# Hybrid decoder block: the input of the first product is loaded in column pieces and turned by TensorE instead of VectorE

## Chip, cores and metric

One core of a Trainium2 chip runs one decoder layer for 256 tokens. The metric is the device time of one execution in microseconds (us), as the median of several runs: 1473.47 us over 3 runs (1473.1 to 1473.87) before the change.

## What is computed

The reference, cut to the part that the change touches and what follows it (sizes: 256 tokens, model width 2048, w_in 2048 x 8704):

```python
u = rms_norm(h, g_mix[l])                      # h is x, (1, 256, 2048)
proj = u @ w_in[l]
q, k, v, z, gb, gc, gate_a, gate_c = jnp.split(proj, split_points, axis=-1)
q = rope(q.reshape(b, t, N_Q_HEADS, HEAD_DIM), positions)
k = rope(k.reshape(b, t, N_KV_HEADS, HEAD_DIM), positions)
y_attn = sliding_window_attention(q, k, v, attn_sinks[l]) @ w_attn_proj[l]
y_conv = short_gated_conv(z, gb, gc, conv_w[l]) @ w_conv_proj[l]
merged = jax.nn.sigmoid(gate_a) * y_attn + jax.nn.sigmoid(gate_c) * y_conv
h = h + merged @ w_mix_out[l]
h = h + cross_attention(rms_norm(h, g_xattn[l]), rms_norm(mem, g_mem[l]), ...)
hid = rms_norm(h, g_ffn[l]) @ w_ffn_in[l]
h = h + (silu(hid[..., :FFN_HIDDEN]) * hid[..., FFN_HIDDEN:]) @ w_ffn_out[l]
```

## The kernel before

Every weight matrix goes through the chip once, in tiles of two contraction blocks of 128 rows by 512 columns (`raw`, 512 KB, five buffers). `weights` (line 70) loads a tile on SP's queue (line 80) and `split` (line 54) cuts it into a high part on ScalarE (`whi`, line 55, a cast) and a low part on VectorE (`wlo`, line 56, a subtraction). `gemm_tf` (line 112) multiplies an activation by 512 columns of a weight, token tile by token tile: three products a contraction tile (`part`, lines 122 to 124: high x high, high x low, low x high), two token tiles, 16 contraction tiles, so 96 products of 128x512 for a matrix with 2048 rows. `gemm_ft` (line 86) gives the transposed result with two products (lines 96 and 100). The order of the instructions on each engine comes from a scheduler that runs over the program; `hooks` lets code run ahead of a given weight tile.

The activation `X1` of the first product has to hold features on the partitions, as a high and a low part, times the gain `g_mix`. Before, x is loaded by `x_in` / `stage_in` (line 227) in eight pieces of 256 KB, each for 32 partitions, such that a partition holds 32 i + b for token 32 j + b and features of block i. VectorE transposes it in squares of 32 x 32 (`feat`, line 214), and `high_low` (lines 221 and 222) makes the high part on ScalarE and the low part on VectorE. Since a partition then holds features m apart, the rows of w_in are loaded to match: `rows_pk` puts row (c P + p) m + k on partition p. `stage_rms` (lines 183 and 235 to 245) makes the tokens' 1/rms from sums of squares on ScalarE, a product with `ones` on TensorE (`ssp`, line 239) and a reduction; `spread` (line 263, tile `rw`) lays it out for later use. `evac_q` (line 297) scales the first product's result by it into `q_sb`.

Ahead of all that TensorE runs 20 matmuls of `ident` with itself (`heat`, line 167). The small constants (`rows`, `rope`, `sink` and the gains, lines 157, 159, 304, 310 and 312) are loaded on SP's queue between the weights; `rows` is turned by TensorE into `cols_ps` (line 306). The first hooks:

```python
first = {k: [lambda k=k: feat(x0, KD, k, 2, k, g_mix, X1)] for k in range(4, KD, 2)}
first[0] = [lambda: x_in(0), lambda: x_feat(0, 0), lambda: x_feat(2, 0)]
first[1] = [lambda: x_in(1), lambda: x_feat(0, 1), lambda: x_feat(2, 1)]
gemm_tf(W, KD, X1, 0, evac_q(0), hooks=first, lead=4, head=2)
```

`lead=4` makes the first four weight tiles one contraction block each (256 KB); `head=2` holds two of them and runs them token tile by token tile.

Of the kernel before, what the change touches and what calls it, by code (L numbers as in the profile page):

```python
# [17 lines left out]
P = 128  # L18
D = 2048
# [22 lines left out]
def hybrid_block(ctx, tc, a, out):  # L42
# [14 lines left out]

    def rows_kp(W):
        """Contraction tile k, partition p holds row k P + p."""
        v = W.rearrange("(k p) n -> p k n", p=P)  # L60
        return lambda k0, n: v[:, k0:k0 + n, :]

    def rows_pk(W, m):
        """Contraction tile m c + k, partition p holds row (c P + p) m + k."""
        v = W.rearrange("(c p k) n -> c p k n", p=P, k=m)
        return lambda k0, n: v[k0 // m][:, k0 % m:k0 % m + n, :]
# [19 lines left out]
    def gemm_ft(W, kt, X, c0, evac, cols=C, hooks=None):  # L86
        """[features, tokens] tiles of X.T @ W[:, c0:c0+cols]; evac first adds the two halves
        of a sum; what it does after its yield is spread over the weight tiles of the next product."""
# [23 lines left out]
    def gemm_tf(W, kt, X, c0, evac, cols=C, hooks=None, last=1, lead=0, head=1):  # L112
        """[tokens, features] tiles of X.T @ W[:, c0:c0+cols]; the first and last weight tiles go token tile by token tile."""
# [40 lines left out]
    def gain(n, m):  # L154
        o = const.tile([P, KD], F32, name=n)
        if m == KD:
            nc.sync.dma_start(o, a[n][0].rearrange("(p k) -> p k", k=m))
        else:
            nc.sync.dma_start(o.rearrange("p (c k) -> p c k", k=m), a[n][0].rearrange("(c p k) -> p c k", p=P, k=m))
        return o  # L160

    g_mix = gain("g_mix", KD)

    # keep the tensor engine's clock up while the first loads are under way
    heat = tps.tile([P, C], F32, tag="tp", name="heat")
    for i in range(20):
        nc.tensor.matmul(heat[:, :P], lhsT=ident, rhs=ident, start=True, stop=True)

    # additive masks: current block keeps key <= query, previous block key > query
# [28 lines left out]
    # A staged block holds 32 i + b on its partitions, for token 32 j + b and features (i, f):  # L198
    # transposing its 32 x 32 squares puts features on the partitions and tokens next to each other.
# [8 lines left out]
    def feat(stage, m, k0, n, kx, g, X, j0=0, nj=NJ):  # L208
        """X[:, kx + k, 0/1, tokens] = high/low parts of (stage * g) for the features f = m a + k0 + k."""
        nt = nj * Q  # L210
        xt = sp.tile([P, n, nt], F32, tag="xt", name="xt", bufs=2)
        v = stage.rearrange("p j (a k) -> p k j a", k=m)
        for k in range(n):
            nc.vector.transpose(xt[:, k, :].rearrange("p (j b) -> p j b", b=Q), v[:, k0 + k, j0:j0 + nj, :])  # L214
        high_low([xt[:, k, :] for k in range(n)], kx, g, X, slice(j0 * Q, j0 * Q + nt))
# [13 lines left out]
    def stage_rms(stage, name):  # L229
        """1/rms of the tokens of a staged block: [P, NT] by partition, and [P, T] on every partition."""  # L230
# [18 lines left out]
    def bounce(c, st, eng=nc.sync):  # L249
        """Stage column chunk c of h by way of DRAM."""  # L250
        hd = dp.tile([T, C], F32, tag="hd", name="hd")
        eng.dma_start(hd.rearrange("(t p) f -> p t f", p=P), h[:, :, c * C:(c + 1) * C])
        for i in range(P // Q):
            stage_in(st, hd, i, eng=eng)

    def spread(r, name):
        """rB[p, t*P + n] = r[n, t] on every partition p."""
# [12 lines left out]
    # ================= mixer =================  # L270
    with ExitStack() as ph:
        mp = ph.enter_context(tc.tile_pool(name="mp", bufs=1))
        ap_ = ph.enter_context(tc.tile_pool(name="ap", bufs=2))
        W = rows_pk(a["w_in"][0], KD)
        x0 = mp.tile([P, NJ, C], F32, tag="x0", name="x0")
        X1 = xp.tile([P, KD, 2, T], F32R, tag="X", name="X1")

        HJ = NJ // 2

        def x_in(th):  # L280
            for i in range(P // Q):
                stage_in(x0, a["x"][0], i, th * HJ, HJ)

        def x_feat(k0, th):
            feat(x0, KD, k0, 2, k0, g_mix, X1, th * HJ, HJ)

        first = {k: [lambda k=k: feat(x0, KD, k, 2, k, g_mix, X1)] for k in range(4, KD, 2)}
        first[0] = [lambda: x_in(0), lambda: x_feat(0, 0), lambda: x_feat(2, 0)]
        first[1] = [lambda: x_in(1), lambda: x_feat(0, 1), lambda: x_feat(2, 1)]
# [3 lines left out]
        def evac_q(c):  # L293
            def evac(t, p):
                if not r0:
                    r0.extend(stage_rms(x0, "r0B"))
# [4 lines left out]
        gemm_tf(W, KD, X1, 0, evac_q(0), hooks=first, lead=4, head=2)  # L301
        NR = 3 * KC
        rows = const.tile([NR, P], F32, name="rows")
        nc.sync.dma_start(rows, a["conv_w"][0].rearrange("j (r c) -> (j r) c", c=P))
# [5 lines left out]
        nc.sync.dma_start(rope, a["rope_table"].rearrange("(t p) s d -> p t s d", p=P))  # L310
        sink = const.tile([P, NH], F32, name="sink")
        nc.sync.dma_start(sink, a["attn_sinks"].broadcast_to([P, NH]))
# [11 lines left out]
        # rotary, in place, on GpSimd  # L324
# [20 lines left out]
        # gated short convolution, [features, tokens]  # L345
# [44 lines left out]
        # attention stages per kv head  # L390
# [26 lines left out]
        def scores(g):  # L417
            kv = g
            p_sb = ap_.tile([P, 4, 3, P], F32, tag="p_sb", name="p_sb")
            # block layout on axis 2: 0 = tile 0, 1..2 = tile 1 (previous, current)  # L420
# [92 lines left out]
        # merge  # L513
# [38 lines left out]
    # ================= cross attention =================  # L552
# [135 lines left out]
    # ================= feed-forward =================  # L688
# [98 lines left out]
```

## Time and profile before

| | |
|---|---|
| median of 3 runs | 1473.47 us (1473.1 to 1473.87) |
| span of the profiled execution | 1474.0 us (the page gives no other time of it) |
| TensorE (PE) busy | 1441.9 us, 98% |
| VectorE (DVE) busy | 886.3 us, 60% |
| ScalarE (ACT) busy | 724.0 us, 49% |
| GpSimd (POOL) busy | 46.6 us, 3% |
| DMA | 275.11 MB, mean 187 GB/s |

The profile is of one execution. Busy shares are means over the whole span; what happens in a stretch is read from the timeline and the windows of that stretch. A busy PE is one that has a matmul in it, at either of its clock levels; the granted clock stands in the windows' column PEclk. PEld is PE's weight load, SPq and POOLq are the queues that issue DMAs.

### The profile page before, as it was taken

How to read it: one execution, taken by the hardware profiler on the slowest of the kernel's cores; microseconds unless marked ns; L12 is line 12 of the kernel's file. 1: busy time of each engine (PE TensorE's matmuls, PEld its weight loads, DVE VectorE, ACT ScalarE, POOL GpSimd, SP SyncE). 2: the span in 40 equal slices, each digit the busy share in tenths (PEclk: the TensorE clock that was granted, in tenths of full speed). 3: DMA queues.
4: the chain of work that ended last, by engine and by line, in shares of the span. 5: the costliest groups of instructions: out<-in, count | busy, mean ns of one | idle time of the engine just before them, and what ended most of it. 6: DMA issues, size and time to landing. Idle time of an engine off the chain costs nothing.

```text
span 1474.0 us, 20189 instructions
## 1 busy us (share of the span) xinstructions
PE 1441.9 (98%) x7707; PEld 1227.6 (83%) x7707; DVE 886.3 (60%) x1316; ACT 724.0 (49%) x1115; POOL 46.6 (3%) x67
## 2 busy tenths in 40 slices
PE   7999999999999996999999999999999999999997
PEld 6888888888888875899888888888888888888886
DVE  6557768555557858585655656556556555545454
ACT  6443555554455545565654544545445444434343
POOL 0061000000000010000000000000000000000000
PEclk9999999999999998999999999999999999999999
DMA  8664454456656678865566665665666666555553
GB/s 227 198 188 147 145 170 148 155 176 198 191 176 192 194 204 241 254 192 163 175 186 186 186 195 183 194 188 186 193 190 184 190 193 217 187 188 189 191 188 115
DMA packets 147028, 275.11 MB, mean 187 GB/s; under 512 B 10588, under 2 KB 18804, under 8 KB 146804
## 3 DMA queue, kind: packets, MB, share of 16 engines
q1 hardware_dynamic: 145780, 269.64, 59.3%
q0 software_dynamic: 1152, 4.19, 1.2%
q8 instruction: 60, 0.98, 0.3%
q14 instruction: 36, 0.29, 0.1%
HBM read 269.60 MB, written 4.19 MB: 186 GB/s over the span
## 4 chain that ended last, share of the span: by engine, by line
PE 92%; DMA 2%; POOL 2%; DVE 2%; issue 1%; ACT 0%; ACTq 0%; POOLq 0%; SPq 0%; DVEq 0%
PE acc L96 41%; PE acc L100 21%; PE acc L123 9%; PE acc L124 9%; PE acc L122 9%; DMA mem<-in_mem 2%; DMA x<-in_x 1%; DVE xt L214 1%; PE sps L430 1%; PE ops L483 1%; DVE XM L222 0%; DVE wlo L56 0%; PE tp L472 0%; POOL sa L336 0%; POOL sa L335 0%
## 5 line engine op out<-in xcount | busy, mean ns | idle before, releaser
L56 DVE TENSOR_TENSOR wlo<-raw,whi 128x1024 fp32r<-128x1024 f32 (+1 forms) x506 | 607.0, 1205 | 527.1 <-ACT whi L55 526.9
L55 ACT CAST whi<-raw 128x1024 fp32r<-128x1024 f32 (+1 forms) x506 | 520.2, 1033 | 624.5 <-PE acc L96 359.7
L96 PE MATMUL acc<-X,whi 128*128 128x512 f32 x2368 | 805.8, 396 | 0.0
L100 PE MATMUL acc<-X,wlo 128*128 128x256 f32 x2368 | 607.3, 280 | 0.0
L96 PEld LDWEIGHTS acc<-X,whi 128*128 128x128 f32 x2368 | 435.9, 188 | 83.6 <-issue 0.8
L100 PEld LDWEIGHTS acc<-X,wlo 128*128 128x128 f32 x2368 | 446.2, 188 | 23.9 <-issue 1.1
L124 PE MATMUL acc<-whi,gT 128*128 128x512 f32 x352 | 138.9, 395 | 0.0
L123 PE MATMUL acc<-wlo,gT 128*128 128x512 f32 x352 | 138.9, 394 | 0.0
L122 PE MATMUL acc<-whi,gT 128*128 128x512 f32 x352 | 125.4, 395 | 0.0
L107 ACT COPY half<-acc 128x256 f32<-128x256 f32 x184 | 67.5, 369 | 25.5 <-PE acc L100 23.5
L122 PEld LDWEIGHTS acc<-whi,gT 128*128 128x128 f32 x352 | 66.4, 189 | 15.5
L124 PEld LDWEIGHTS acc<-whi,gT 128*128 128x128 f32 x352 | 66.3, 188 | 15.5
L123 PEld LDWEIGHTS acc<-wlo,gT 128*128 128x128 f32 x352 | 66.3, 188 | 15.4
L123 PE MATMUL acc<-wlo,MG 128*128 128x512 f32 x128 | 51.0, 399 | 12.7 <-DVE wlo L56 12.7
L124 PE MATMUL acc<-whi,MG 128*128 128x512 f32 x128 | 50.6, 395 | 0.0
L122 PE MATMUL acc<-whi,MG 128*128 128x512 f32 x128 | 45.4, 393 | 0.0
L96 PE MATMUL acc<-yc,whi 128*128 128x512 f32 x128 | 43.7, 394 | 0.0
L96 PE MATMUL acc<-oT,whi 128*128 128x512 f32 x128 | 43.5, 394 | 0.0
L122 PE MATMUL acc<-whi,X 128*128 128x512 f32 x96 | 34.4, 401 | 5.9 <-ACT whi L55 3.3
L123 PEld LDWEIGHTS acc<-wlo,MG 128*128 128x128 f32 x128 | 24.5, 192 | 18.7 <-DVE wlo L56 13.5
L123 PE MATMUL acc<-wlo,X 128*128 128x512 f32 x96 | 38.2, 403 | 0.9 <-DVE wlo L56 0.9
L124 PE MATMUL acc<-whi,X 128*128 128x512 f32 x96 | 37.6, 397 | 0.0
(189 smaller groups left out, 1106.1 us busy)
## 6 DMA issues: line engine op xcount, KB each, us to landing
raw<-in_w_ffn_in SPq DMA_DIRECT2D x176, 512.0 KB, 4.3
raw<-in_w_in SPq DMA_DIRECT2D x134, 512.0 KB, 3.8
raw<-in_w_ffn_out SPq DMA_DIRECT2D x88, 512.0 KB, 4.6
raw<-in_w_mix_out SPq DMA_DIRECT2D x32, 512.0 KB, 4.8
raw<-in_w_attn_proj SPq DMA_DIRECT2D x16, 512.0 KB, 4.3
raw<-in_w_conv_proj SPq DMA_DIRECT2D x16, 512.0 KB, 4.0
raw<-in_w_xkv SPq DMA_DIRECT2D x8, 512.0 KB, 3.9
raw<-in_w_xkv SPq DMA_DIRECT2D x16, 256.0 KB, 2.8
```

Of the source, the lines that this page charges most:

```text
L55: nc.scalar.copy(hi, src)
L56: nc.vector.tensor_tensor(out=lo, in0=src, in1=hi.bitcast(F32), op=ALU.subtract)
L96: nc.tensor.matmul(ps[m], lhsT=hi[:, k, ms], rhs=X[:, kk].rearrange("p s t -> p (s t)"), start=(kk == 0), stop=False,)
L100: nc.tensor.matmul(ps[m][:, :T], lhsT=lo[:, k, ms], rhs=X[:, kk, 0, :], start=False, stop=(kk == kt - 1),)
L107: nc.scalar.copy(t2, ps[m][:, T:])
L122: nc.tensor.matmul(o, lhsT=xh, rhs=hi[:, k, :cols], start=(kk == 0), stop=False)
L123: nc.tensor.matmul(o, lhsT=xh, rhs=lo[:, k, :cols], start=False, stop=False)
L124: nc.tensor.matmul(o, lhsT=xl, rhs=hi[:, k, :cols], start=False, stop=(kk == kt - 1))
L214: nc.vector.transpose(xt[:, k, :].rearrange("p (j b) -> p j b", b=Q), v[:, k0 + k, j0:j0 + nj, :])
L430: nc.tensor.matmul(sps[par][:, j].rearrange("p a b -> p (a b)"), lhsT=qT[b:b + 64, hh // 2, t * P:(t + 1) * P], rhs=kT[b:b + 64, sw, kv // ...
L483: nc.tensor.matmul(ops[64 * par:64 * par + 64], lhsT=v_sb[:, kb, vs], rhs=pt[:, t + kb, par::2, :], start=(kb == 0), stop=(kb == t),)
```

## The change

x is loaded with tokens on the partitions, all 128 of them, in column pieces: 256, 256, 512, 512 and 512 columns of both token tiles, each issued on SP between the first weight tiles. TensorE transposes the 128 x 128 blocks into PSUM (`x_turn`), two contraction tiles a PSUM tile, and `high_low` reads PSUM. The gain g_mix is loaded as 16 rows on ScalarE's queue and turned by TensorE as well. Sums of squares are taken from the natural layout (`x_sums`), so that `ssp` goes. w_in is read by `rows_kp`: tile k holds the neighbouring rows k P to k P + 127. `heat` has 8 matmuls instead of 20, `head=2` goes, and the other small loads move from SP's queue to GpSimd's. The rest of the kernel stays.

```diff
     def gain(n, m):
         o = const.tile([P, KD], F32, name=n)
         if m == KD:
-            nc.sync.dma_start(o, a[n][0].rearrange("(p k) -> p k", k=m))
+            nc.gpsimd.dma_start(o, a[n][0].rearrange("(p k) -> p k", k=m))
         else:
-            nc.sync.dma_start(o.rearrange("p (c k) -> p c k", k=m), a[n][0].rearrange("(c p k) -> p c k", p=P, k=m))
+            nc.gpsimd.dma_start(o.rearrange("p (c k) -> p c k", k=m), a[n][0].rearrange("(c p k) -> p c k", p=P, k=m))
         return o
-    g_mix = gain("g_mix", KD)
+    g_rows = const.tile([KD, P], F32, name="g_rows")
+    nc.scalar.dma_start(g_rows, a["g_mix"][0].rearrange("(k p) -> k p", p=P))
     heat = tps.tile([P, C], F32, tag="tp", name="heat")
-    for i in range(20):
+    for i in range(8):
         nc.tensor.matmul(heat[:, :P], lhsT=ident, rhs=ident, start=True, stop=True)
...
-        W = rows_pk(a["w_in"][0], KD)
-        x0 = mp.tile([P, NJ, C], F32, tag="x0", name="x0")
+        W = rows_kp(a["w_in"][0])
+        x0 = mp.tile([P, NT, D], F32, tag="x0", name="x0")
         X1 = xp.tile([P, KD, 2, T], F32R, tag="X", name="X1")
-        HJ = NJ // 2
-        def x_in(th):
-            for i in range(P // Q):
-                stage_in(x0, a["x"][0], i, th * HJ, HJ)
-        def x_feat(k0, th):
-            feat(x0, KD, k0, 2, k0, g_mix, X1, th * HJ, HJ)
-        first = {k: [lambda k=k: feat(x0, KD, k, 2, k, g_mix, X1)] for k in range(4, KD, 2)}
-        first[0] = [lambda: x_in(0), lambda: x_feat(0, 0), lambda: x_feat(2, 0)]
-        first[1] = [lambda: x_in(1), lambda: x_feat(0, 1), lambda: x_feat(2, 1)]
+        xn = a["x"][0].rearrange("(t p) d -> p t d", p=P)
+        ss0 = tiny.tile([P, NT, D // C], F32, tag="ss0", name="ss0")
+        g_mix = const.tile([P, KD], F32, name="g_mix")
+        def x_in(f0, f1):
+            nc.sync.dma_start(x0[:, :, f0:f1], xn[:, :, f0:f1])
+        def g_turn():
+            gp = tps.tile([P, C], F32, tag="tp", name="gp")
+            nc.tensor.transpose(gp[:, :KD], g_rows, ident[:KD, :KD])
+            nc.vector.tensor_copy(g_mix, gp[:, :KD])
+        def x_turn(k):
+            tp = tps.tile([P, 2, T], F32, tag="tp", name="tp")
+            for i in range(2):
+                for t in range(NT):
+                    nc.tensor.transpose(
+                        tp[:, i, t * P:(t + 1) * P], x0[:, t, (k + i) * P:(k + i + 1) * P], ident)
+            high_low([tp[:, i, :] for i in range(2)], k, g_mix, X1)
+        def x_sums(c):
+            for t in range(NT):
+                sumsq(x0[:, t, c * C:(c + 1) * C], ss0[:, t, c:c + 1])
+        first = {k: [] for k in (0, 1, 2, 3, 4, 6, 8, 10, 12, 14)}
+        first[0] = [lambda: x_in(0, 2 * P), g_turn, lambda: x_turn(0)]
+        first[1] = [lambda: x_in(2 * P, C), lambda: x_turn(2)]
+        first[3] = [lambda: x_in(C, 2 * C)]
+        first[4] = [lambda: x_turn(4), lambda: x_turn(6), lambda: x_in(2 * C, 3 * C)]
+        first[6] = [lambda: x_sums(0)]
+        first[8] = [lambda: x_turn(8), lambda: x_turn(10), lambda: x_in(3 * C, D)]
+        first[10] = [lambda: x_sums(1)]
+        first[12] = [lambda: x_turn(12), lambda: x_turn(14), lambda: x_sums(2)]
+        first[14] = [lambda: x_sums(3)]
...
                 if not r0:
-                    r0.extend(stage_rms(x0, "r0B"))
+                    r = rstd_sum(ss0)
+                    r0.extend((r, spread(r, "r0B")))
...
-        gemm_tf(W, KD, X1, 0, evac_q(0), hooks=first, lead=4, head=2)
+        gemm_tf(W, KD, X1, 0, evac_q(0), hooks=first, lead=4)
...
-        nc.sync.dma_start(rows, a["conv_w"][0].rearrange("j (r c) -> (j r) c", c=P))
+        nc.gpsimd.dma_start(rows, a["conv_w"][0].rearrange("j (r c) -> (j r) c", c=P))
...
-        nc.sync.dma_start(rope, a["rope_table"].rearrange("(t p) s d -> p t s d", p=P))
+        nc.gpsimd.dma_start(rope, a["rope_table"].rearrange("(t p) s d -> p t s d", p=P))
...
-        nc.sync.dma_start(sink, a["attn_sinks"].broadcast_to([P, NH]))
+        nc.gpsimd.dma_start(sink, a["attn_sinks"].broadcast_to([P, NH]))
```

The scheduler's order at the places that matter. SP's queue from the start of the program, before (x is the input tile, raw a weight tile; a row is the line, the kind and the transfer's shape):

```order
L157 DMA g_mix<-in_g_mix 128x16
L227 DMA x_129<-in_x 32x4x512 x4
L80 DMA raw<-in_w_in 128x512
L227 DMA x_129<-in_x 32x4x512 x4
L80 DMA raw<-in_w_in 128x512 x3
L80 DMA raw<-in_w_in 128x2x512
L304 DMA rows<-in_conv_w 24x128
```

and of the change:

```order
L284 DMA x_117<-in_x 128x2x256
L80 DMA raw<-in_w_in 128x512
L284 DMA x_117<-in_x 128x2x256
L80 DMA raw<-in_w_in 128x512 x2
L284 DMA x_117<-in_x 128x2x512
L80 DMA raw<-in_w_in 128x512
L284 DMA x_117<-in_x 128x2x512
L80 DMA raw<-in_w_in 128x2x512 x2
L284 DMA x_117<-in_x 128x2x512
```

The first weight tile moves from behind 1 MB of x to behind 256 KB of it, and the last piece of x to behind eight contraction tiles of weights.

ACT's queue at the same place, before (junk is a sum of squares, X a high part of the activation, whi a high part of a weight):

```order
L183 ACTIVATE junk,ssj<-x_129 128x512
L221 ACTIVATE X_130<-xt,g_mix 128x128 x2
L183 ACTIVATE junk,ssj<-x_129 128x512
L221 ACTIVATE X_130<-xt,g_mix 128x128
L55 CAST whi<-raw 128x512
```

and of the change:

```order
L55 CAST whi<-raw 128x512
L185 ACTIVATE junk,ss_119<-x_117 128x512 x2
L55 CAST whi<-raw 128x512 x2
L223 ACTIVATE X_118<-tp,g_mix 128x256 x2
L185 ACTIVATE junk,ss_119<-x_117 128x512
L223 ACTIVATE X_118<-tp,g_mix 128x256
L185 ACTIVATE junk,ss_119<-x_117 128x512
L223 ACTIVATE X_118<-tp,g_mix 128x256 x2
```

Two sums of squares and three casts now stand ahead of the first X. PE's queue of the change, from its first matmul (gp is the turned gain, tp the turned x, acc a product; before, the 20 matmuls of heat are followed by products alone):

```order
L169 MATMUL heat<-ident 128x128 x8
L288 MATMUL gp<-ident,g_rows 128x16
L295 MATMUL tp<-ident,x_117 128x128 x8
L122 MATMUL acc<-whi,X_118 128x512
L123 MATMUL acc<-wlo,X_118 128x512
L122 MATMUL acc<-whi,X_118 128x512
L123 MATMUL acc<-wlo,X_118 128x512
L295 MATMUL tp<-ident,x_117 128x128 x4
```

Eight of the 32 transposes stand ahead of the first product, the others in groups of four between the products. After the first gemm the rows of all engines are the same as before, line numbers aside.

## Rows read from the trace of the kernel before

**Rows 1.** The page: span, and the chain that ended last, by engine

```profile
span 1474.0 us, 20189 instructions
...
PE 92%; DMA 2%; POOL 2%; DVE 2%; issue 1%; ACT 0%; ACTq 0%; POOLq 0%; SPq 0%; DVEq 0%
```

**Rows 2.** Timeline of PE, first 20 us: start, duration, engine, line, what, count, [idle before]

```profile
1.53 7.20 PE L167 MATMUL heat<-ident 128*128 128x128 f32 x40 [1.53 <-POOL ident masks.py:199]
11.99 0.51 PE L122 MATMUL acc<-whi,X 128*128 128x512 f32 x1 [3.25 <-ACT whi L55]
```

**Rows 3.** Windows: stretch, length, busy time by engine, granted clock, DMA share, GB/s

```profile
15.00:20.00 5.00, 3.86 (x8) 2.34 (x9) 4.71 (x13) 4.31 (x12) 0.00 (x0) 0.50 1.06 307
...
1.53:8.73 7.20, 7.20 (x40) 1.00 0.87 193
11.99:16.14 4.15, 1.24 (x3) 0.69 1.05 286
16.14:20.20 4.06, 4.06 (x8) 0.50 1.05 273
20.20:41.10 20.90, 20.18 (x89) 1.00 0.72 228
```

**Rows 4.** Waits of the first 45 us: who, for whom, us in total, times, longest

```profile
DVE xt L214 <- DMA x<-in_x: 8.3, 1, 8.3
```

**Rows 5.** Timeline of ACT, first 45 us

```profile
11.33 0.60 ACT L55 CAST whi<-raw 128x512 fp32r<-128x512 f32 x1
12.14 0.61 ACT L183 ACTIVATE junk<-x 128x512 f32<-128x512 f32 x1
12.88 0.63 ACT L183 ACTIVATE junk<-x 128x512 f32<-128x512 f32 x1
41.56 1.27 ACT L297 ACTIVATE q_sb<-acc,rstd 128x512 f32<-128x512 f32 x2 [1.91 <-PE acc L124]
```

**Rows 6.** Timeline of PE, 36 to 45 us

```profile
36.54 0.39 PE L124 MATMUL acc<-whi,X 128*128 128x512 f32 x1
...
37.45 0.39 PE L122 MATMUL acc<-whi,X 128*128 128x512 f32 x1
...
43.34 0.39 PE L123 MATMUL acc<-wlo,X 128*128 128x512 f32 x1
...
44.06 0.50 PE L124 MATMUL acc<-whi,X 128*128 128x512 f32 x1
```

**Rows 7.** DMA: landing times of x (tile x), SP's timeline, issues of weights

```profile
DMA to landing us min/median/max: 4.2/6.5/9.7
...
1.19 1.84 SPq L227 DMA_DIRECT2D x<-in_x  x4
...
raw<-in_w_xkv SPq DMA_DIRECT2D x16, 256.0 KB, 2.8
```

**Rows 8.** Tile tp (transposes through PSUM later in the kernel) and PE's timeline there

```profile
L221 ACT ACTIVATE X<-tp,g_ffn x16: 459/472/477, 718.6 to 740.0; 128x256 fp32r<-128x256 f32 x16
L222 DVE SCALAR_TENSOR_TENSOR X<-tp,g_ffn,X x16: 473/478/485, 719.8 to 740.5; 128x256 fp32r<-128x256 f32 x16
...
717.47 1.35 PE L677 MATMUL tp<-ident,h 128*128 128x128 f32 x10
```

**Rows 9.** DMA issues on POOL's queue: KB each, median us to landing

```profile
mem<-in_mem POOLq DMA_DIRECT2D x4, 512.0 KB, 18.2
```

**Rows 10.** Timelines of POOL and DVE, 525 to 566 us

```profile
532.92 1.19 POOL L227 DMA_DIRECT2D mem<-in_mem  x2
...
559.29 2.08 DVE L214 STREAM_TRANSPOSE xt<-mem 128x256 f32<-128x256 f32 x4 [13.41 <-DMA mem<-in_mem]
```

**Rows 11.** Windows in the mixer, and DMA issues of weights (w_in by rows_pk)

```profile
50.00:100.00 50.00, 50.00 (x242) 42.04 (x241) 22.88 (x18) 22.23 (x25) 14.97 (x21) 1.00 0.62 191
...
raw<-in_w_in SPq DMA_DIRECT2D x134, 512.0 KB, 3.8
...
raw<-in_w_mix_out SPq DMA_DIRECT2D x32, 512.0 KB, 4.8
```

## Prediction

> **What bounds the kernel now.** I read the page first. Of a span of 1474.0 us, the chain that ended last is 92% TensorE (PE) [rows 1]. So a time is worth something only where PE stands still or is slowed, and the place to look is where the change is: the start. The timeline of PE's first microseconds shows it: warming matmuls ("heat") until 8.73, then nothing until the first product (a 128x512 matmul of the first gemm) at 11.99 [rows 2]. The windows show what follows: three products up to 16.14, busy 1.24 of 4.15 us, then eight in 4.06, twice the later pace. Their clock column has granted 1.00 over 1.53 to 8.73, 0.69 from 11.99 to 16.14, 0.50 (the 1.2 GHz level) from 16.14 to 20.20, and 1.00 after that [rows 3]. The waits of the first 45 us name the cause: DVE stands 8.3 us for the DMA of x [rows 4], ACT's cast of the first weight (whi) ends only at 11.93 [rows 5], and PE's first product is released by it [rows 2]. From 20.20 to 41.10 PE is busy 20.18 of 20.90 us [rows 3].
>
> How much is lost: the marker is the start of ACT's q_sb (line 297), which releases when the first product's first token tile is complete: 41.56 [rows 5]. The first gemm has 96 products up to about there (16 contraction tiles, 3 products, 2 token tiles). In the steady stretch four starts take 0.91 us, 0.2275 each [rows 6], so 96 are 21.8 us. From 11.99 to 41.56 is 29.6: 7.7 us are holes, half clock, and the two passes of the ssp product. Everything behind the marker is bound by PE in both kernels.
>
> **The change, step by step.** All of it is at the start; the order excerpts show what stands on SP, ACT and PE. Behind the first gemm, the instructions of every engine stand in the same order as before.
>
> *Loads.* Before, SP issues eight pieces of x (256 KB each, 32 partitions) around one weight tile. They land 4.2 to 9.7 us after issue, the ninth issue of 0.46 from 1.19 on ending at about 5.4, so x is complete at about 15.1, and from 1.53 to 8.73 the DMA engines move 193 GB/s at a share of 0.87; from 15 to 20, with weights alone, 307 GB/s at 1.06 [rows 3, 7]. Per share, x costs about 1.3 times as much. Now x comes over 128 partitions, as weights do, the first piece being 256 columns (256 KB). I have no row for such a piece of x. Bounds for its landing: 2.8 us (w_xkv, 256 KB over 128 partitions, same row length) and 4.2 us (the fastest piece of x before) [rows 7]. I take 3.1, near the first, because shape and bytes are those of w_xkv. Four issues on SP take 1.84, 0.46 each, from 1.19 on; x's first now takes g_mix's place, one ahead, at 0.74 [rows 7]; the pieces are then bound by their bytes at 307 GB/s, 0.85 us for 256 KB. Landings: x0 3.85, w0 4.7, x1 5.55, w1 6.4, w2 7.25, then 512 KB of x at 9.0, w3 9.8, x 11.5, w4-5 13.2.
>
> *First product.* ACT's new order decides: cast of w0, two sums of squares of x (which need x1), casts of w1 and w2, and only then X of tile 0. Cast 0.60; squares 0.74 each where they follow each other (12.14 to 12.88) [rows 5]; X from PSUM 0.472 [rows 8]. So 4.7+0.60 = 5.3; squares 5.55 to 7.05; casts to 8.25; X at 8.7; with 0.06 to PE (11.93 to 11.99 in rows 2 and 5) the first product starts at **8.8 instead of 11.99**. Heat is 8 matmuls instead of 20 (40 passes took 7.20, so 16 take some 3.2 and end by 4.9); the first eight transposes follow it and are done near 6.5, hidden under ACT's casts. If that cover were gone they would cost 8 x 0.18 = 1.4 at heat's mean pace.
>
> *PE after its first product.* 96 products 21.8. 24 more transposes of 128x128: ten of them stand between 717.47 and 718.57, 0.11 each, and I take 0.12: 2.9. The DVE's 20 transposes of x go, which PE did not pay for directly. The two transposes of the spread (rw) and cols_ps move ahead of the marker: 43.34 to 44.06 holds them and one product [rows 6], so they are 0.5, paid before the marker and saved behind it. The ssp product goes (two passes); I leave its gain as reserve against small new waits.
>
> *Waits that it adds.* X of the two columns in one PSUM tile alternates ACT 0.472 and DVE 0.478 [rows 8], about 1.0 a column; behind the first X, ACT does X, a sum of squares, X, a sum, X: X of contraction tile 3 at 8.7 + 3x0.47 + 2x0.74 = 11.6, while PE has 18 products and 4 transposes (4.6 us) before it needs that, 13.4. So short holes only: bounds 0.3 and 2.0, taken 1.0. ACT has 16 X, 8 sums, 4 short and 6 long casts, some 22 us from 4.7 on, which ends near 27 and leaves it ahead of PE.
>
> *Clock.* Before, it fell while PE had stood still for 3.3 us and then run three products, and it was back at 20.2 after products had run back to back from 16.14 [rows 2, 3]. Now PE stands still from 6.5 to 8.8 and is broken up until 12. Bounds: no loss, or a half clock for as long as before: a mean of 0.69 over 4.15 us is 2.6 us at half, and with the 4.06 behind it [rows 3] 6.6, of which half is lost, 3.3. Taken 1.6, the middle. The Trainium skill ("TensorE: Matmul & The Clock Gate", Part 4) states that transposes do not count as activity for the clock; no row before shows transposes alone at a start. By that rule the loss is the upper bound and the result 1469.7, by the middle 1468.0.
>
> *Small loads.* rows, rope, sink and three gains go to POOL's queue, where a load of 512 KB takes 18 us to land [rows 9]. The first user is cols_ps, which the new order puts among the last products of the first gemm, near 33; issued at about 3 they have 30 us. Cost nothing; without that cover PE would stand at cols_ps until they land. They share the DMA engines with x; before, they did that at 12 to 17 us. The gain g_mix is loaded on ACT's queue, idle then, and turned by PE in one small transpose, under the wait for x.
>
> *Sum to the marker.* 8.8 + 21.8 + 2.9 + 0.5 + 1.0 + 1.6 = 36.6, that is 5.0 earlier than 41.56, and 0.5 more is saved behind it: **5.5 us**. Nothing takes it back: the long wait at 559 is for mem, whose loads POOL issues at 532.0 when the mixer's tiles come free, so it moves along [rows 10]. The page gives only the span of the profiled execution, 1474.0, against a median of 1473.47 over the runs; 5.5 off each gives 1468.5 of span and **1468.0 us** for the runs.
>
> **Rivals.**
> 1. *The clock stays low from the first product on until products have run for long.* For: only 8 heat matmuls, then transposes, then a hole. Against: the engine is loaded from 1.53 to 6.5. Price 3.3 instead of 1.6, at most 4.5 if it is low from 8.8 to 17.8: 1469.7 to 1470.9. The rule named above leads here.
> 2. *x comes no faster than before.* The pieces have 1 KB and 2 KB runs; if the first lands after 4.2 and each 256 KB of x takes 1.2 us as before (5.4 to 15.1 for eight pieces), x1 lands at 6.95, the first product starts at 10.2, 1.4 later, and w4-5 lands at 16.0. ACT casts it behind two squares, to 17.6, DVE's low part (1.2) is there at 18.8, and PE asks for it after 24 products and 12 transposes, at 17.1: 1.7 more. 3.1 in all: 1471.1. Against: weights over 128 partitions move at 307 GB/s.
> 3. *Slower.* w_in's tiles now read 128 neighbouring rows each (a stride of one row, 34.8 KB) instead of every sixteenth. If this slowed each transfer, all 138 loads of w_in would be hit. The point: PE eats 512 KB in 12 products, 2.73 us, 192 GB/s, and the share of the DMA engines is 0.62 at that [rows 11], so nothing happens until transfers take 1.6 times as long; at 1.7 times, 134 x 2.73 x 0.05 = 18 us: 1486. Against: w_mix_out is already read so and lands in 4.8 us, w_in in 3.8 the old way [rows 11]: 1.26 times at most, no sign of 1.6.
>
> **How the numbers follow.** Forecast 0.68, rival 1 0.17, rival 2 0.10, rival 3 0.05. Low end: no clock loss (1.6), holes of 0.3 (0.7), first landing at 2.8 (0.3): 2.6 under, 1465.4. High end: clock 3.3 (1.7), first landing at 4.2 (1.1), holes near 2.0 (0.8): 3.6 over, 1471.6, which takes in rivals 1 and 2. 0.2% is 2.9 us, about what a measurement of this kernel can tell from no change: faster means under 1470.5. The forecast (all but 0.03 of it), four fifths of rival 1 and 0.02 of rival 2 are there: faster 0.81; rival 3 is slower, 0.05; the rest, 0.14, is within.
>
> **What would show it.** First product near 8.8 (wrong if after 10.5); q_sb near 36.6; some 3 us of products at half clock after it; x's pieces landing in 3 to 4 us; the windows from 45 us on equal to the old ones; w_in still landing in about 4 us; DVE's wait for mem still 13 us. The forecast is wrong if q_sb is earlier by under 2 or over 8 us, or if PE has holes in the mixer behind 45 us.

## The result, and the profile after

The change makes the kernel faster: 1456.63 us median (1455.4 to 1459.74, 4 executions) against 1473.67 (1473.1 to 1476.33, 4 executions), a ratio of 0.9881 with a 95% interval of 0.9865 to 0.9896. That is 17 us, three times the 5.5 forecast, and outside the range that was given (1465.4 to 1471.6).

The page of the changed kernel shows a span of 1453.6 us and the same chain as before, PE from end to end:

```profile
span 1453.6 us, 20169 instructions
...
PE 93%; POOL 2%; DMA 2%; DVE 2%; issue 1%; ACT 0%; SPq 0%; ACTq 0%; POOLq 0%; DVEq 0%
```

The two profiled spans differ by 20.4 us, more than the medians do, since each is one execution: the one after is the fastest of its four (1455.4 us of time for 1453.6 of span), and an execution of the kernel before with a span of 1474.0 took 1476.03 us in a later set, 2.4 above the median above. The ledger below is that of the two spans.

**The start** did nearly what the prediction said. The timeline of PE's first microseconds after the change (columns as in rows 2):

```profile
1.54 3.78 PE L169 MATMUL heat<-ident 128*128 128x128 f32 x16 [1.54 <-POOL ident masks.py:199]
...
5.47 1.80 PE L295 MATMUL tp<-ident,x 128*128 128x128 f32 x8
9.05 0.50 PE L122 MATMUL acc<-whi,X 128*128 128x512 f32 x1 [1.79 <-ACT X L223]
```

Here the first product starts at 9.05, released by ACT's first X. The windows behind it (columns as in rows 3, with ACT and POOL busy):

```profile
9.05:10.51 1.46, 1.46 (x9) 1.24 (x9) 1.08 (x3) 1.19 (x4) 0.00 (x0) 0.95 1.09 253
10.51:13.94 3.43, 3.43 (x10) 2.71 (x9) 2.12 (x5) 3.25 (x10) 0.00 (x0) 0.52 1.01 382
13.94:36.00 22.06, 22.06 (x109) 18.07 (x108) 15.38 (x25) 13.56 (x24) 0.73 (x1) 1.00 0.80 259
```

PE has no hole between 9.05 and 36.00, and runs 3.43 us at a granted clock of 0.52. The marker, from ACT's timeline, and the landing of x, from the view of that tile:

```profile
36.00 1.27 ACT L321 ACTIVATE q_sb<-acc,rstd 128x512 f32<-128x512 f32 x2 [1.89 <-PE acc L124]
```

```profile
DMA to landing us min/median/max: 3.2/6.3/10.0
```

So the marker is 5.6 us earlier than in [rows 5].

**The rest of the gain lies where the two programs have the same instructions in the same order.** Four places hold it.

1. Windows around PE's pause of 2 us at 112 us (before) and 106 us (after): before the change PE then runs at half clock, here not. Before, then after:

```profile
112.60:116.00 3.40, 3.40 (x13) 2.81 (x12) 3.40 (x7) 0.00 (x0) 3.40 (x4) 0.50 0.51 148
```

```profile
112.60:116.00 3.40, 3.40 (x23) 3.00 (x22) 2.74 (x3) 1.05 (x1) 0.55 (x1) 1.00 0.63 161
```

That is 1.7 us, and no run credits it to the change: a_start below, which has the change's start, is granted 0.66 from 108 to 112, behind the same pause, and b_sink, which has the old start, 1.00 behind its own. Each kernel was profiled once, so what decides it is not shown.

2. The loads of h and mem. The timelines of DVE (the last product that frees the mixer's tiles), POOL (the issue that waits for it) and DVE again (the first use of mem), before:

```profile
528.73 0.42 DVE L529 TENSOR_TENSOR s<-s,sa 128x256 f32<-128x256 f32 x1
...
532.01 0.91 POOL L577 DMA_DIRECT2D h<-in_x  x1 [414.06 <-issue]
```

and after:

```profile
520.97 0.42 DVE L553 TENSOR_TENSOR s<-s,sa 128x256 f32<-128x256 f32 x1
...
522.13 0.79 POOL L601 DMA_DIRECT2D h<-in_x  x1 [408.97 <-ACT MG L55]
...
545.32 2.09 DVE L216 STREAM_TRANSPOSE xt<-mem 128x256 f32<-128x256 f32 x4 [5.16 <-DMA mem<-in_mem]
```

Before, the issue comes 2.9 us after the end of DVE's product, and after the change 0.7. DVE's wait for mem is 5.2 us instead of the 13.4 of [rows 10]. PE stands for it too, because the low part of the next weight (wlo) comes behind mem's transposes in DVE's queue. The timeline of PE, before and then after:

```profile
563.13 0.80 PE L123 MATMUL acc<-wlo,MG 128*128 128x512 f32 x1 [11.49 <-DVE wlo L56]
```

```profile
544.93 0.73 PE L122 MATMUL acc<-whi,MG 128*128 128x512 f32 x2 [1.62 <-ACT whi L55]
549.16 0.79 PE L123 MATMUL acc<-wlo,MG 128*128 128x512 f32 x1 [3.50 <-DVE wlo L56]
```

The landing of mem, from the view of that tile, before and after:

```profile
DMA to landing us min/median/max: 12.5/18.2/23.8
```

```profile
DMA to landing us min/median/max: 8.7/14.8/19.7
```

The first use of mem is 14.0 us earlier than before. DVE's product, which releases the load, is already 7.8 us earlier: 5.6 of the marker, 1.7 of the pause, and 0.5 that come from tiles' places (item 3). So 6.2 us arise here: 2.1 because the issue follows sooner on its release, and 4.1 because the last piece of mem lands 19.7 us after its issue instead of 23.8.

3. The last stage, w_ffn_out. The rows of its products by tile gT (ns min/median/max of one, first and last start), before and after:

```profile
L122 PE MATMUL acc<-whi,gT x352: 387/393/404, 1219.5 to 1464.2; 128*128 128x512 f32 x176
```

```profile
L122 PE MATMUL acc<-whi,gT x352: 389/389/398, 1205.1 to 1443.8; 128*128 128x512 f32 x176
```

The stage takes 244.7 us before and 238.7 after: 6.0 us. The windows with that tile alone say it as products in 200 us of a PE that is never idle at full clock, before and after:

```profile
1240.00:1440.00 200.00, 200.00 (x862) 162.17 (x861) 0.00 (x0) 0.00 (x0) 1.00 0.59 189
```

```profile
1240.00:1440.00 200.00, 200.00 (x884) 165.58 (x884) 0.00 (x0) 0.00 (x0) 1.00 0.59 183
```

The pitch, the time from the start of one product to the start of the next, is 0.232 us before and 0.226 after (most starts are 0.227 apart, the figure that the expectations below use). The mixer's last products, by tile oT, show the same on a smaller scale, 78.5 us from first to last start before and 77.9 after:

```profile
L96 PE MATMUL acc<-oT,whi x128: 387/396/401, 433.8 to 512.3; 128*128 128x512 f32 x128
```

```profile
L96 PE MATMUL acc<-oT,whi x128: 387/391/403, 426.7 to 504.6; 128*128 128x512 f32 x128
```

That is the 0.5 of item 2.

4. Between the first use of mem and the last stage 0.4 us. The sum: 5.6 + 1.7 + 0.5 + 6.2 + 0.4 + 6.0 = 20.4.

What the change did to these stages without touching their code can be read from the two programs. It allocates two more tiles, so that what lies behind them in a partition moves: g_rows (512 bytes, ahead of all the large tiles) and ss0 (128 bytes for four buffers, behind the weight tiles). In both kernels X, raw, whi and wlo start 224 bytes past a multiple of 256, while h, mem, oT, yc, XM, xo and gT start 96 past one before and 224 past one after. And it gives POOL's queue six loads at the start; before, h's load was POOL's first.

### The profile page after: what moved, and what is told of

Same layout as the page of the kernel before. It is cut to its first block, busy times and chain, and to the rows that moved or that the text cites. A ratio compares the mean times of both kernels' runs of the same rounds, so it can differ in the third digit from the quotient of the medians.

```text
span 1453.6 us, 20169 instructions
## 1 busy us (share of the span) xinstructions
PE 1433.3 (99%) x7714; PEld 1226.3 (84%) x7714; DVE 878.2 (60%) x1291; ACT 723.6 (50%) x1111; POOL 51.5 (4%) x73
## 4 chain that ended last, share of the span: by engine, by line
PE 93%; POOL 2%; DMA 2%; DVE 2%; issue 1%; ACT 0%; SPq 0%; ACTq 0%; POOLq 0%; DVEq 0%
PE acc L96 42%; PE acc L100 21%; PE acc L123 9%; PE acc L124 9%; PE acc L122 9%; DMA h<-in_x 1%; PE sps L454 1%; DVE xt L216 1%; PE ops L507 1%; DVE XM L224 0%; PE tp L496 0%; DMA raw<-in_w_in 0%; POOL sa L359 0%; POOL sa L362 0%; DVE wlo L56 0%
## 5 line engine op out<-in xcount | busy, mean ns | idle before, releaser
L124 PE MATMUL acc<-whi,gT 128*128 128x512 f32 x352 | 136.9, 389 | 0.0
L122 PE MATMUL acc<-whi,gT 128*128 128x512 f32 x352 | 123.4, 389 | 0.0
L107 ACT COPY half<-acc 128x256 f32<-128x256 f32 x184 | 67.4, 369 | 25.2 <-PE acc L100 22.9
L197 POOL TENSOR_TENSOR rstd<-ms,mhalf 128x2 f32<-128x2 f32 (+1 forms) x6 | 6.0, 998 | 927.5 <-DVE ms L195 927.5
```

The costliest lines, as they stand in the source:

```text
L107: nc.scalar.copy(t2, ps[m][:, T:])
L122: nc.tensor.matmul(o, lhsT=xh, rhs=hi[:, k, :cols], start=(kk == 0), stop=False)
L124: nc.tensor.matmul(o, lhsT=xl, rhs=hi[:, k, :cols], start=False, stop=(kk == kt - 1))
L197: nc.gpsimd.tensor_tensor(out=r, in0=ms, in1=mhalf[:, :n], op=ALU.pow)
```

## The experiments

All times are medians, each beside the kernel before on the same chip.

| kernel | us | before | ratio (95%) |
|---|---|---|---|
| changed kernel | 1456.63 | 1473.67 | 0.9881 (0.9865 to 0.9896) |
| b_pad: before, gT 128 bytes on | 1462.41 | 1473.56 | 0.9923 (0.9906 to 0.9939) |
| a_pad: changed, gT 128 bytes on | 1463.33 | 1473.56 | 0.9926 (0.9907 to 0.9945) |
| b_pool: before, small loads on POOL | 1469.51 | 1473.56 | 0.9970 (0.9959 to 0.9982) |
| a_sp: changed, small loads on SP | 1461.75 | 1473.56 | 0.9913 (0.9894 to 0.9931) |
| a_start: changed, start alone | 1468.83 | 1474.30 | 0.9960 (0.9947 to 0.9973) |
| b_memset: before, one memset more | 1469.86 | 1474.30 | 0.9963 (0.9948 to 0.9978) |
| b_sink: before, sink on POOL | 1467.86 | 1474.30 | 0.9955 (0.9940 to 0.9969) |
| a_c32: changed, all 32 bytes on | 1456.34 | 1474.30 | 0.9865 (0.9848 to 0.9882) |
| a_w64: changed, X and weights 64 apart | 1466.37 | 1474.27 | 0.9947 (0.9932 to 0.9962) |
| a_heat12: changed, 12 of heat | 1458.69 | 1474.27 | 0.9894 (0.9877 to 0.9910) |
| a_mem: changed, mem ahead of h | 1455.33 | 1474.27 | 0.9873 (0.9858 to 0.9887) |
| b_both: before, sink on POOL and gT on | 1462.85 | 1475.27 | 0.9919 (0.9905 to 0.9932) |

**Where gT lies: b_pad and a_pad.** Both get this edit:

```diff
     nc.gpsimd.memset(ones, 1.0)
+    pad = tiny.tile([P, 32], F32, tag="pad", name="pad", bufs=1)
+    nc.gpsimd.memset(pad, 0.0)
```

> The kernel before with one unused 128-byte tile in the pool tiny, which moves every tile behind it (h, mem, oT, yc, XM, xo, gT) by 128 bytes; X, raw, whi and wlo stay. Theory A (the pitch of the last stage's products hangs on where gT starts: 96 bytes past a multiple of 256 before, 224 past one in the changed kernel): products of w_ffn_out start 0.227 us apart instead of 0.232, 5.5 us less in that stage, and the time is about 1468. Theory M (the shorter wait for mem comes from the new place of h and mem in the buffer): DVE's wait for mem falls from 13.4 to about 5 us, 8 more, 1460. Rival (both come from something else, such as the timing handed on from the start): pitch 0.232, wait 13, time 1473.5.

> The changed kernel with the same 128-byte tile: gT starts 96 bytes past a multiple of 256 again, like before the change, though at another place. Theory A: pitch in the last stage back to 0.232, 5.5 to 6 us longer than the changed kernel, about 1462. Theory M: the wait for mem back to about 13 us as well. Rival: pitch stays at 0.227 and the time at 1456.6.

The same window of the last stage, b_pad and then a_pad:

```profile
1240.00:1440.00 200.00, 200.00 (x884) 165.69 (x883) 0.00 (x0) 0.00 (x0) 1.00 0.62 192
```

```profile
1240.00:1440.00 200.00, 200.00 (x863) 162.33 (x862) 0.00 (x0) 0.00 (x0) 1.00 0.59 183
```

The pitch follows the place in both directions, with the code of the start left as it was: theory A holds, and gT's place is worth 6 us (the memset that both edits add is left out in a_start and b_both below, with the same outcome). b_pad gained 11 us, though, not 5.5: its wait for mem fell to 6.7 us as well, as theory M said. But a_pad, with mem's old place modulo 256, kept a short wait (5.0 us; its ratio is worse than the changed kernel's by 0.0045, 6.6 us, of which its last stage has 6.0). So the place of mem is not it, and b_pad holds something else: its memset on POOL, which the next runs take apart.

**POOL's queue: b_pool and a_sp.** The edits move the loads of `rows`, `rope`, `sink` and the gains (not g_mix) between queues. One line of b_pool's edit; a_sp turns all such lines of the changed kernel back:

```diff
-        nc.sync.dma_start(sink, a["attn_sinks"].broadcast_to([P, NH]))
+        nc.gpsimd.dma_start(sink, a["attn_sinks"].broadcast_to([P, NH]))
```

> The kernel before with its small loads (rows, rope, sink, three gains; g_mix stays) on POOL's queue. Theory P (the first DMA that POOL issues in a program takes longer to start, 2.3 us from the last semaphore event against 0.6, and later ones don't): the h and mem loads at 532 start 1.7 us sooner after their release, and DVE's wait for mem falls by 2 to 8 us; time 1466 to 1472. Rival (queue does not matter for mem): wait 13.4, time 1473 to 1474. The pitch of the last stage stays at 0.232 under both.

> The changed kernel with its small loads back on SP's queue (g_mix's rows stay on ACT's). Theory P: POOL's first load is again that of h near 522, starts 1.7 us later after its release, and the wait for mem grows from 5.2 us by 2 to 8; time 1458.5 to 1465. Rival: wait 5 us, time 1456 to 1458 (the small loads then cost SP seven issues of 0.46 us each between weights at the start).

b_pool gained 4 us with the pitch at 0.232 and a wait of 3.6 us for mem, a larger fall than the 2 to 8 expected; a_sp lost some 5 against the changed kernel, with a wait of 12.5: the queue of the small loads does matter for mem, 500 us later. But theory P, as put, was already hit by b_pad, where h's load is POOL's first and is yet issued 0.6 us after its last semaphore event.

**What delays the issue: b_memset and b_sink.** One memset more (b_memset), and one load alone on POOL's queue (b_sink, the line shown above):

```diff
     nc.gpsimd.memset(ones, 1.0)
+    nc.gpsimd.memset(ones, 1.0)
```

> The kernel before with one more memset on POOL (ones, a second time): all tiles stay where they are, the order on other engines too. Theory F (POOL fetches its next 8 KB of instructions between the release of h's load and its issue, at 530.3; one instruction more moves that fetch elsewhere): no such fetch near 530, h is issued 0.6 us after POOL's last semaphore event instead of 2.3, xt of mem comes 2 to 4 us earlier against the start of w_mix_out's products, time 1469.5 to 1472. Rival (first use of the queue is what takes the 1.7 us): nothing moves, 1473.5.

> The kernel before with the load of sink alone (8 KB) on POOL's queue. Theory Q (POOL's queue needs 1.2 us or more for its first transfer beyond what later ones need: first packet 2.7 to 3.7 us after the issue of h in the runs where POOL had issued nothing, 1.5 in those where it had): first packet of h 1.5 us after its issue, and xt of mem 31 us after the start of w_mix_out's products instead of 37.5, time 1466.5 to 1470. Rival (it takes all six loads, or is something else): first packet at 2.7 or later, time above 1471.

The view of the DMA queues in the microseconds around the issue shows the cause. The kernel before, 529 to 533, and b_memset, 528.5 to 531 (queue, kind: packets, MB, share):

```profile
q1 hardware_dynamic: 339, 0.66, 52.4%
q14 instruction: 1, 0.01, 0.6%
```

```profile
q1 hardware_dynamic: 145, 0.26, 29.8%
```

Before the change a packet of instructions (8 KB, at 530.3) is fetched between the release of the load and its issue; a_sp and a_start show the same packet at that place, and b_memset, b_pad and all kernels with loads on POOL at the start don't. In b_memset it stands 413 us earlier instead, at the start of POOL's wait; its queues from 116 to 118, where the kernel before has no such packet:

```profile
q14 instruction: 1, 0.01, 1.3%
```

So one instruction more moves the border of the fetched block to the other end of the wait. b_memset's issue at 529.35 is 2.7 us earlier than before, 2.1 of them between DVE's product and the issue (0.8 instead of 2.9); the other 0.6 its execution had from its start on. Its wait and landing are:

```profile
  DMA mem<-in_mem: 5.5, 1
DMA to landing us min/median/max: 9.0/15.5/20.6
```

Theory F holds. The first use of mem is 5.9 us earlier (553.43 instead of 559.29), 5.3 without those 0.6, more than the 2 to 4 expected: 2.1 of the sooner issue and 3.2 of a shorter way to the last landing (20.6 us instead of 23.8). What shortens the landing was not tried alone. That the later issue puts more of SP's weights ahead of mem is an argument, for which the queues speak: in the 2.5 us from h's issue on, q1, the queue of SP's loads, moves 0.69 MB before and 0.16 in b_memset.

The first packet on POOL's queue q0 is a second, smaller part. The queues in the 2.5 us from h's issue on, b_memset and then b_sink:

```profile
q1 hardware_dynamic: 85, 0.16, 24.2%
```

```profile
q0 software_dynamic: 32, 0.13, 27.7%
q1 hardware_dynamic: 57, 0.10, 10.1%
```

Where POOL has issued nothing before, no packet of its queue moves within 2.5 us (2.6 to 3.7 in the five kernels of that kind); where it has, the first moves after 1.5. b_sink's wait is 4.2 us and its last landing 19.4. Its median is 2 us under b_memset's, but the two intervals overlap, so a gain in time by this part is not shown. The page "DMA: Bandwidth & Descriptors" of the Trainium skill (Specifications) gives the first byte of a POOL transfer about 1 us; the runs show 1.5, and more for a queue's first. On the fetch, the page "Runtime: NRT & Kernel Launch" of the Trainium skill (Instruction fetch mechanics) holds that the cost of crossing a block is mostly hidden; here it was not, behind a wait that had just ended.

**The start alone: a_start.** a_sp, with ss0 doubled so that gT lies at its slow place and no instruction is added:

```diff
-        ss0 = tiny.tile([P, NT, D // C], F32, tag="ss0", name="ss0")
+        ss0 = tiny.tile([P, 2 * NT, D // C], F32, tag="ss0", name="ss0")[:, :NT, :]
```

> The changed kernel stripped to its start: small loads back on SP (g_mix's rows stay on ACT), and 128 bytes more behind ss0 without any instruction, so that gT starts 96 bytes past a multiple of 256 as before the change. If the forecast was right about the part it spoke of, and the rest of the gain is a matter of addresses and of POOL's queue: q_sb 2.7 to 5.5 us earlier than before (38.9 in the run with the loads on SP), pitch 0.232, mem awaited as before, time 1466 to 1470. Rival (the start is worth more than its marker shows): below 1464.

1468.83, 5.5 us under the kernel before on the same chip; the interval of the ratio makes that 4.0 to 7.8 us. The slow pitch (862 products in the window of the last stage) and the wait for mem (13.2 us) are back. Its marker, 39.52, is 2.0 us earlier, less than the 2.7 to 5.5 expected, and a poor measure: PE starts some ten products more ahead of it than in the changed kernel, since the scheduler put products of the second token tile there. At the mixer's last products (tile oT) it leads by 4.6 us. Before the change, and a_start:

```profile
L96 PE MATMUL acc<-oT,whi x128: 387/396/401, 433.8 to 512.3; 128*128 128x512 f32 x128
```

```profile
L96 PE MATMUL acc<-oT,whi x128: 387/396/401, 429.2 to 507.7; 128*128 128x512 f32 x128
```

At the last start of tile gT the lead is 4.8 us, in a profile of the slowest of its five executions. So the part of which the forecast spoke came out within a microsecond of it.

**Place or distance: a_c32 and a_w64.** 32 bytes more behind ident move everything; 64 between the pools xp and wp move the weight tiles and what follows, but not X:

```diff
-    ident = const.tile([P, P], F32, name="ident")
+    ident = const.tile([P, P + 8], F32, name="ident")[:, :P]
```

```diff
+    gap = ctx.enter_context(tc.tile_pool(name="gap", bufs=1))
+    gap.tile([P, 16], F32, name="gap64")
     wp = ctx.enter_context(tc.tile_pool(name="wp", bufs=2))
```

> The changed kernel with 32 bytes more behind ident, which puts X, raw, whi, wlo, gT and the rest at multiples of 256 bytes instead of 224 past one. Theory D (what counts is the distance between the stationary and the moving operand modulo 256): nothing moves, pitch 0.227 in the last stage, time 1456.6. Theory L (operands that start 32 bytes off a multiple of 64 cost extra reads): pitch below 0.227 in the last stage and below 0.348 for a pair in the products with a weight as the stationary operand; by some 0.005 each 20 us less, about 1436. Theory S (224 past a multiple of 256 is a good place and 0 is not): pitch 0.232 again, 1462 or more.

> The changed kernel with 64 unused bytes between X and the weight tiles: raw, whi, wlo and everything behind them (gT too) move by 64 bytes, X stays. So gT and whi keep a distance of a multiple of 256 bytes, X and whi get one of 64 more. Theory D (the distance between stationary and moving operand modulo 256 sets the pitch: 0 gives 0.227, 128 gives 0.232): last stage stays at 0.227; products of w_in and w_mix_out with X and MG as the stationary operand slow from 0.227 to something up to 0.232, pairs with a weight as the stationary operand from 0.348 upwards; time 1457 to 1470. Rival (the place of gT alone counts, not its distance to whi): the last stage changes its pitch, since gT now starts at 32 past a multiple of 256. Rival 2 (only 128 matters): time as the changed kernel, 1456.6.

a_c32 is as fast as the changed kernel (1456.34), with 884 products in the window of the last stage: gT may lie at a multiple of 256 or 224 past one. a_w64 shows the rest. Its two windows (last stage, and w_ffn_in's 800 to 1100), then the second of the changed kernel:

```profile
1240.00:1440.00 200.00, 200.00 (x884) 165.64 (x884) 97.75 (x86) 81.36 (x86) 0.00 (x0) 1.00 0.63 194
800.00:1100.00 300.00, 300.00 (x1707) 261.67 (x1706) 172.78 (x239) 144.42 (x211) 0.00 (x0) 1.00 0.64 187
```

```profile
800.00:1100.00 300.00, 300.00 (x1724) 262.30 (x1723) 176.03 (x248) 147.56 (x220) 0.00 (x0) 1.00 0.65 189
```

gT, moved together with whi to 32 past a multiple, keeps 884; the stages where X stayed and whi moved are 1% slower, and the time is 10 us longer (2 of them at the start, where its marker is 38.05). Theory D holds at the three distances tried: 0, 64 and 128 modulo 256. At 64 both operands lay at places that were fast in other pairs (224 and 32). The distance 128 was tried only with gT and its neighbours at 96 past a multiple, so for them that place as such is not ruled out.

**Two tries to go on: a_heat12 and a_mem.**

```diff
-    for i in range(8):
+    for i in range(12):
         nc.tensor.matmul(heat[:, :P], lhsT=ident, rhs=ident, start=True, stop=True)
```

```diff
-            if c < 2:
-                hooks[8] = [lambda: stage_in(mem, a["mem"][0], 2 * c, eng=nc.gpsimd)]
-                hooks[12] = [lambda: stage_in(mem, a["mem"][0], 2 * c + 1, eng=nc.gpsimd)]
-            else:
+            if c == 0:
+                hooks[8] = [lambda i=i: stage_in(mem, a["mem"][0], i, eng=nc.gpsimd) for i in (0, 1)]
+                hooks[12] = [lambda i=i: stage_in(mem, a["mem"][0], i, eng=nc.gpsimd) for i in (2, 3)]
+            if c >= 2:
```

> The changed kernel with 12 matmuls of heat instead of 8. Heat ends at 5.9 us instead of 5.3, the first eight transposes follow to 7.5, and PE's first product waits for ACT until 9.0 as before. If PE's half clock between 9 and 14 us (in some executions: q_sb at 34.5 without it, 36.0 and 37.7 with it) hangs on the pause ahead of the first product, it becomes rarer: q_sb near 34.5 to 35, median 1455 to 1456. Rival (the clock falls as often): 1456 to 1458.

> The changed kernel with the four loads of mem directly behind the first piece of h on POOL's queue, ahead of the other three pieces of h (order before: h, mem, mem, h, mem, mem, h, h). 512 KB less stand ahead of the last piece of mem; four pieces and h's first then land some 3 to 4 us earlier. The scheduler now puts mem's first transposes one weight earlier in DVE's queue, which takes 2.7 us of that back. Expected if the wait for mem is what PE stands for at 545: 1 to 3 us less, 1454 to 1456. Rival (the loads share one rate, so that order moves nothing): 1456.6 or more.

a_heat12 missed and says nothing of the clock: the scheduler, with heat longer, put DVE's copy of the turned gain behind three weights, and PE stood for it. From its timeline of PE:

```profile
10.65 0.66 PE L295 MATMUL tp<-ident,x 128*128 128x128 f32 x4 [3.42 <-DVE g_mix L289]
11.71 0.79 PE L122 MATMUL acc<-whi,X 128*128 128x512 f32 x1 [0.41 <-ACT X L223]
```

a_mem has the lowest median of all, 1455.33, inside what was expected; its interval overlaps that of the changed kernel, so that a gain over it is not shown. Mem's last piece lands 17.8 us after issue instead of 19.7, but DVE asks for it one weight earlier.

**The side effects without the change: b_both.** b_sink, with ssj doubled as ss0 was (128 bytes, no instruction):

> The kernel before with only two edits that touch nothing of its start: the load of sink on POOL's queue, and 128 unused bytes behind ssj (no instruction), so that gT, and with it h, mem, oT, yc, XM and xo, keep a distance of a multiple of 256 bytes to whi. Theory: the changed kernel's gain beyond its start is these two things, and they add up: 6.0 us in the last stage (pitch 0.227), 6 to 7 us at the wait for mem; q_sb stays near 41.5; time 1461 to 1462.5. Rival (they share a cause or cancel in part): above 1464. The rest to the changed kernel, 5 to 6 us, is then the start.

1462.85 against 1475.27, 12.4 us, with the marker at 41.56 as before. That is 0.35 longer than the 1461 to 1462.5 expected, which is within its spread (1462.16 to 1463.86). The two edits, which leave the start alone, add up to what the forecast had missed: 12.4 and a_start's 5.5 make 17.9, where the change gave 17.

## Why the prediction was wrong, and where it was right

*What bounds the kernel now.* Right for the start, wrong in its last sentence: "Everything behind the marker is bound by PE in both kernels." PE-bound it was, but at a pitch that is not a constant; and at 551 to 563 us PE stood for mem in a way that an earlier issue could shorten.

*Loads.* First piece 3.2 us (taken 3.1). The later ones took up to 10.0, where 3 to 4 was named as a sign; they were hidden behind the casts.

*First product.* 9.05 against 8.8 forecast. Heat's 16 passes took 3.78 instead of 3.2 us and the eight transposes ended at 7.27 instead of 6.5; both lay under ACT's work, as said.

*PE after its first product, waits, clock.* From the first product to the marker 26.95 us, against 27.8 in the sum. No holes (1.0 taken), and 3.43 us at a granted clock of 0.52, which is 1.65 lost (1.6 taken). What is left, 25.3, is the sum's 25.2 for products and transposes. Behind the marker 0.2 more came, where 0.5 was forecast: ACT's cast at 47.38 is at 41.62 after the change. The loss is no fixed size: a_pad's window from 9 to 14 us shows 1.00 and its marker is 34.54, a_c32's from 8.5 to 15 shows 0.50 and its marker is 37.66.

```profile
9.00:14.00 5.00, 5.00 (x24) 3.88 (x25) 3.39 (x8) 4.45 (x13) 0.00 (x0) 1.00 1.04 344
```

```profile
8.50:15.00 6.50, 5.21 (x14) 4.22 (x15) 4.22 (x8) 5.52 (x15) 0.00 (x0) 0.50 1.06 376
```

Both bounds of the term were met, by kernels with the same order on PE. What the prediction cites of the Trainium skill on transposes and the clock is neither borne out nor refuted by them.

*Small loads: the step that failed.* "Cost nothing" asked what the six loads would suffer on POOL's queue, and not what they would do to it. They made h's load no longer POOL's first and moved the border of the instruction fetch; with that, the step "the long wait at 559 is for mem, [...] so it moves along" fell: the wait went from 13.4 to 5.2 us. b_sink shows 6.4 us for it, by one load (4.6 to 8.8 by the interval).

*The step that was not there.* "Behind the first gemm, the instructions of every engine stand in the same order as before" was taken to mean the same time. The sum has no term for where tiles lie. Two new small tiles moved gT, and its 1056 products got shorter by 0.0057 us each, 6.0 us. b_pad, a_pad, a_start and b_both show it.

*Rivals.* Of the three, the first two concerned the start, and none had the sign of what happened. The loss of the first, 3.3 us, came about in a_c32 (6.5 us at half clock), but not here (1.65); the first product at 10.2 of the second did not come. The third, a slower stream of w_in, did not come: its loads land in 4.3 us (3.8 before), and PE has no hole in the mixer but the pause that it had.

In sum: the forecast of 5.5 us was right for the start (a_start: 5.5, between 4.0 and 7.8), and wrong for the kernel, because 12 of 17 us came from two side effects that no part of the sum asked about. That the start agrees to the tenth is luck: the holes that were taken and did not come are a microsecond, and the clock cost from nothing to about its upper bound in kernels with the same order on PE.

## What to carry to other kernels

Ask of every change what it moves without naming it: the addresses of all tiles allocated behind a new one, and the state of each queue and instruction stream that it uses for the first time. When a trace shows the same instruction at two pitches in two stages (here 0.226 and 0.232 us), that difference is a price that any change of layout can pay or collect; compare the distance of the two operands before calling later stages untouched. To credit a gain to its cause, build the change without its side effects and the side effects without the change: here they add up, and 128 unused bytes and one moved load are worth more than the redesign of the start.

## What the runs showed of the hardware

- A 128x512 product takes 0.226 us when its stationary and moving operand start at a distance of 0 modulo 256 bytes in their partitions, and 0.232 at 128; at 64, w_ffn_in's products, of 512 and 256 columns, ran 1% slower (1707 in 300 us, not 1724). The absolute place (0, 32 and 224 past a multiple of 256, each at the distance 0) made no difference; the distance 128 was seen only with gT and its neighbours at 96. Why was not tried.
- POOL's issue of a load was held 1.7 us longer by a fetch of 8 KB of instructions that fell right behind the end of a wait of 412 us; one memset more in POOL's program moved it to the other end of the wait and took 4.4 us off the kernel.
- Where h's load was the first that POOL's queue carried, its first packet came 2.6 to 3.7 us after the issue (five kernels); where the queue had carried a load at the start, 1.5 (the nine others).
- A pause of PE of about 2 us is followed by 3.4 us at half clock in some kernels (before, b_pad, b_memset, a_start) and by none in others (changed kernel, b_sink), with the same instructions there, one profile of each.
